# The last two pairs' operands queued behind the last token tile's finish, and its transposes behind the next stage's first product

## The chip, the cores and the metric

The kernel runs on one core of a Trainium2 chip. Its time is device microseconds (us) of one execution, and less is better. TensorE (PE) multiplies, VectorE (DVE) and ScalarE (ACT) work elementwise, GpSimd (POOL) does small operations and issues some DMAs, SyncE (SP) issues most DMAs. Each engine runs its instructions in the order in which they stand in its queue.

## The reference, cut to what matters

The reference is a trunk of two layers on 1024 tokens by 1024 channels in fp32.

```python
h = x
for i in range(DEPTH):
    ...
    if i % N_MIXERS == 0:
        mix = s5_mixer(hn, ...)          # state-space scan, then z @ w_glu, val * sigmoid(gate)
    else:
        mix = shortconv_mixer(hn, ...)   # u @ w_in, gated width-3 conv, @ w_out
    h = h + mix
    h = h + swiglu_ffn(rmsnorm(h, norm_ffn_g[i]), ffn_w_in[i], ffn_w_out[i])
    gate = jax.nn.sigmoid(rmsnorm(h, norm_ple_g[i]) @ ple_w_gate[i])
    h = h + gate * (p[i] @ ple_w_up[i])
return rmsnorm(h, final_norm_g)
```

Ahead of each product stands a norm over the channels, and the product contracts over channels. So the normed tokens have to be transposed before they can be an operand.

## The kernel before, in words

The 1024 tokens are eight tiles of 128, taken in the order 0, 4, 1, 5, 2, 6, 3, 7 (`ORDER`). The last token tile is therefore tile 7. A fp32 product is made of three matmuls of high and low halves (`mm3`, L121 to L124). A high half is an ACT cast (L87), a low half is a DVE subtraction behind it (L88).

**A stage that ends in a norm.** Its products give a tile's `h` (L502 and L503 in `glu`, L433 and L435 in `ple`, L360 in `out_phase`). `square` (L139) sums squares on ACT, `norm_stat` (L144 to L148) makes the factor `rs`, POOL computing the power, and `normed` (L173, DVE) writes the normed tile `xn`. Then PE transposes `xn` in two halves of four 128x128 blocks each (`transposed`, L181).

**A pair.** Three of the stages that follow a norm (the first FFN's input, the convolution's input, the second FFN's input) use `block_product`, seven products for a 2 by 2 block product. Its seven moving operands `c` = 0 to 6 are made by `norm_pair(q)` from tiles `q` and `q + 4`: `c` = 0 and 3 are the two halves of tile `q`, 5 is a half of tile `q + 4`, and 1, 2, 4, 6 are differences T2, T1, T3, T4 (L221 to L232). Each takes a cast and a subtraction. Operands 1 and 2 of the last pair need T1 and T2, and those need the transposes of tile 7. `weights_set` makes seven weight operands `ws` out of two raw loads of 512 KB each (`ra` and `rb`): L275, L276, L278 and L283 are its DVE differences, of which L275 needs both loads.

**The order.** `post(t)` runs after tile t. Before, it runs pair 0 after tile 1, pair 1 after tile 2, pair 2 (tiles 2 and 6) after tile 3, and pair 3 (tiles 3 and 7) after tile 7. A scheduler with priorities orders each engine's queue; `first()` raises an instruction's priority. Products of a block are written 0, 1, 2, 3, ..., and PE's queue takes 0, then 3, then the first matmul each of 1 and 2.

**Slots.** Raw weight loads, the `xn` of the paired stages and the chunks `ch` of hidden activations (one for each token tile in `out_phase`, L346) share four buffers, and they take turns in the order of the program:

```python
if i is None:
    slots.append(slots.pop(0))
```

So a new tile takes the buffer of the fourth allocation before it, and its load waits until the last reader of that one is done. SP issues these loads in its queue's order. `spill` (L236) writes `h` back to DRAM from POOL's queue.

In this document the three places are called S1 (`glu` to the first FFN's input, 400 to 430 us), S2 (`ple` to the convolution's input, 1200 to 1236 us) and S3 (`conv_out`, an `out_phase`, to the second FFN's input, 1545 to 1580 us).

Of the kernel before, what the change touches and what calls it, by code (L numbers as in the profile page):

```python
# [23 lines left out]
def trunk(  # L24
# [107 lines left out]
    def square(t, cs):  # L132

        if "ms" not in squares:
            squares["ms"] = tiny.tile([P, T, 4], F32, name="ms", tag="ms")
        got = squares.setdefault(t, [])
        junk = t2_tile("junk", BF16, D)
        ms = squares["ms"][:, t, len(got):len(got) + 1]
        A.activation(junk[:, cs], h[t][:, cs], AF.Square, scale=1.0 / math.sqrt(D), accum_out=ms)  # L139
        got.append(ms)  # L140

    def norm_stat(t):
# [62 lines left out]
        return uhigh[:, c - 4, kt, l, :]  # L205

    def norm_pair(q, gb):
        t0, t1 = q, q + HT
        halves = 2 if q == HT - 1 else 1
        x0, x1 = normed(t0, gb, halves), normed(t1, gb, halves)  # L210

        def put(c, src):
            split(moving_part(c, 0, q), moving_part(c, 1, q), by_kt(src))

        p11, p12, p22 = transposed(x0, 0), transposed(x1, 0), transposed(x1, 1)
        p21 = transposed(x0, 1, mm)
        put(0, p11)
        b12 = t2_tile("b12")
        A.copy(b12, p12)
        T1 = t2_tile("T1")  # L220
        V.tensor_tensor(T1, b12, p11, ALU.subtract)  # L221
        T2 = t2_tile("T2")
        V.tensor_tensor(T2, p22, T1, ALU.subtract)
        put(1, T2)
        put(2, T1)
        put(3, p21)
        T3 = t2_tile("T3")
        V.tensor_tensor(T3, p22, b12, ALU.subtract)
        put(4, T3)
        put(5, p22)  # L230
        T4 = t2_tile("T4")
        V.tensor_tensor(T4, p21, T2, ALU.subtract)  # L232
        put(6, T4)

    def spill(t):
        nc.gpsimd.dma_start(out=hdram[t], in_=h[t])  # L236
# [52 lines left out]
    def block_product(ws, on_c11=None):  # L289


        def prod(ps, i, start):
            for kt in range(KH):
                sl = slice(kt * P, (kt + 1) * P)
                mm3(ps, ws[i][:, 0, sl], ws[i][:, 1, sl], moving(i, kt, 0), moving(i, kt, 1),
                    start and kt == 0, kt == KH - 1, more=not start)

        a = psum()
        prod(a, 0, True)
        s1 = ev_tile("s1")  # L300
# [25 lines left out]
    def out_phase(wout, groups, last_post, following=()):  # L326
# [6 lines left out]
        for gi, group in enumerate(groups):  # L333
# [5 lines left out]
            for t in ORDER:  # L339
# [10 lines left out]
                for j in parts:  # L350
                    mine = [x[0] for x in group if x[0] // 4 == j]
                    for nb in range(2):
                        cs = slice(nb * 512, (nb + 1) * 512)
                        for ht in mine:
                            ch = parts[j][:, ht % 4]
                            bhi, blo = (w[:, cs] for w in units[ht])
                            mm3(ps[nb], ch[:, 0], ch[:, 1], bhi, blo, ht == group[0][0], ht == group[-1][0])
                        if mine[-1] == group[-1][0]:
                            with first():
                                V.tensor_tensor(h[t][:, cs], ps[nb], h[t][:, cs], ALU.add)  # L360
                                if last:
                                    square(t, cs)
                if soon:
# [52 lines left out]
    def ple(l, units, post):  # L416
        more, makers = ple_units(l, 1, [room_new(i) for i in range(4)])
        for nb in range(2):
# [3 lines left out]
            for t in ORDER:  # L422
# [3 lines left out]
                for c0, c1 in ((0, 256), (256, 512)) if last else ((0, 512),):  # L426
# [4 lines left out]
                    with first():  # L431
                        A.activation(ps, ps, AF.Sigmoid)
                        V.tensor_tensor(upt[:, c0:c1], ps, upt[:, c0:c1], ALU.mult)  # L433
                        hc = slice(nb * 512 + c0, nb * 512 + c1)
                        V.tensor_tensor(h[t][:, hc], upt[:, c0:c1], h[t][:, hc], ALU.add)  # L435
                        square(t, hc)
                if nb == 0 and makers:
                    makers.pop(0)()
# [42 lines left out]
    def glu(post):  # L481
# [3 lines left out]
        for nb in range(4):  # L485
# [8 lines left out]
            for t in ORDER:  # L494
# [5 lines left out]
                with first():  # L500
                    A.activation(sg, ps[:, 256:512], AF.Sigmoid)
                    V.tensor_tensor(sg, ps[:, 0:256], sg, ALU.mult)  # L502
                    V.tensor_tensor(h[t][:, cs], sg, h[t][:, cs], ALU.add)  # L503
                    square(t, cs)
                if nb == 3:
                    post(t)
# [503 lines left out]
    def posted(gain, pairs):  # L1010

        gb = load_gain(gain)

        def pair(q):
            norm_pair(q, gb)
            spill(q)
            spill(q + HT)

        def post(t):
            if not pairs:  # L1020
                return norm_tile(t, gb)
            if 0 < t < HT:
                pair(t - 1)
            if t == T - 1:
                pair(HT - 1)
        return post

    def inner(name, make, bufs, extra=()):
# [71 lines left out]
```

## Time and profile before

| What | Value |
|---|---|
| Time, median of 3 runs | 2356.33 us (2354.39 to 2356.82) |
| The profiled execution's own time | 2359.43 us |
| Its span in the profile | 2357.5 us |
| PE busy | 2247.0 us, 95% |
| DVE busy | 1331.9 us, 56% |
| ACT busy | 765.5 us, 32% |
| POOL busy | 163.1 us, 7% |
| DMA | 288.87 MB moved, mean 123 GB/s |

The profiled execution took 3.10 us longer than the median of the runs. Its span lies 1.9 us below its time; that rest lies outside the span. Busy shares are means over the whole span, and a stage can look quite different.

### The profile page before, as it was taken

The numbers are of one execution on the slowest core, as the hardware profiler recorded it, in microseconds if no ns is written. First come the engines' busy times: TensorE is split into PE (matmuls) and PEld (weight loads), VectorE is DVE, ScalarE is ACT, GpSimd is POOL, SyncE is SP. The second block draws the span as 40 slices with busy tenths as digits, with TensorE's granted clock in tenths as the row PEclk, the third lists the DMA queues.
The fourth block names the chain that finished last, engine by engine and source line by source line (L and its number), as shares of the span: only waits on it lengthen the run. The fifth ranks groups of instructions, "written<-read, shape, count | busy, mean of one in ns | idle before, by whom it ended". The sixth has DMA issues, their size and how long they took to land.

```text
span 2357.5 us, 27090 instructions
## 1 busy us (share of the span) xinstructions
PE 2247.0 (95%) x10253; PEld 1835.7 (78%) x10253; DVE 1331.9 (56%) x2246; ACT 765.5 (32%) x1449; POOL 163.1 (7%) x268
## 2 busy tenths in 40 slices
PE   6888999899999999999979999989999999999998
PEld 4776887788888878878858888768888888788787
DVE  7785326866666642125488776487666666121454
ACT  6554223433333320013343332153333333000232
POOL 2110001000000000000000000010000001000000
PEclk8999999999999999999989999999999999999999
DMA  7555202333333364333232225434333335543333
GB/s 246 141 135 148 69 1 89 105 112 112 111 114 110 107 241 149 118 127 114 70 129 81 90 92 179 159 125 125 108 108 107 111 113 172 212 139 107 108 109 110
DMA packets 212978, 288.87 MB, mean 123 GB/s; under 512 B 21360, under 2 KB 152432, under 8 KB 212848
## 3 DMA queue, kind: packets, MB, share of 16 engines
q1 hardware_dynamic: 191520, 212.63, 29.0%
q0 software_dynamic: 20928, 74.47, 10.2%
q8 instruction: 80, 1.31, 0.2%
q14 instruction: 50, 0.41, 0.1%
q10 hardware_dynamic: 400, 0.04, 0.0%
HBM read 190.93 MB, written 79.69 MB: 115 GB/s over the span
## 4 chain that ended last, share of the span: by engine, by line
PE 85%; DMA 6%; DVE 5%; ACT 1%; SPq 1%; issue 1%; POOL 0%; DVEq 0%; POOLq 0%; ACTq 0%
PE psmm L122 27%; PE psmm L124 27%; PE psmm L123 27%; DMA ch<-hid 2%; PE pstr L181 1%; DMA raw<-in_ffn_w_out_dram 1%; DMA tw<-tmp 1%; DVE W L575 1%; DVE gv L925 1%; DMA h<-hd 1%; DVE tmp L575 1%; DVE ulow L88 1%; DVE uhigh L88 1%; PE pstr L874 0%; DVE raw L575 0%
## 5 line engine op out<-in xcount | busy, mean ns | idle before, releaser
L122 PE MATMUL psmm<-ulow,ws 128*128 128x512 f32 x896 | 351.1, 393 | 1.6 <-ACT s L301 1.6
L123 PE MATMUL psmm<-ulow,ws 128*128 128x512 f32 x896 | 350.6, 391 | 0.0
L124 PE MATMUL psmm<-ulow,ws 128*128 128x512 f32 x896 | 350.4, 391 | 0.0
L124 PE MATMUL psmm<-uhigh,ws 128*128 128x512 f32 x672 | 265.3, 395 | 0.0
L122 PE MATMUL psmm<-uhigh,ws 128*128 128x512 f32 x672 | 265.1, 394 | 0.0
L123 PE MATMUL psmm<-uhigh,ws 128*128 128x512 f32 x672 | 264.9, 394 | 0.0
L360 DVE TENSOR_TENSOR h<-psmm,h 128x512 f32<-128x512 f32 x128 | 88.0, 690 | 276.6 <-PE psmm L124 276.6
L88 DVE TENSOR_TENSOR ws<-raw,ws 128x512 fp32r<-128x512 f32 x224 | 153.6, 688 | 117.8 <-ACT ws L87 117.4
L87 ACT CAST ws<-raw 128x512 fp32r<-128x512 f32 x224 | 137.5, 619 | 213.0 <-PE psmm L124 211.2
L122 PEld LDWEIGHTS psmm<-ulow,ws 128*128 128x128 f32 x896 | 169.4, 189 | 39.5 <-ACT s L301 2.9
L123 PEld LDWEIGHTS psmm<-ulow,ws 128*128 128x128 f32 x896 | 169.4, 189 | 36.2
L124 PEld LDWEIGHTS psmm<-ulow,ws 128*128 128x128 f32 x896 | 169.2, 189 | 36.2
L87 ACT CAST ws<-st 128x512 fp32r<-128x512 f32 x168 | 104.0, 620 | 204.4 <-PE psmm L124 189.5
L123 PEld LDWEIGHTS psmm<-uhigh,ws 128*128 128x128 f32 x672 | 126.1, 188 | 30.3
L124 PEld LDWEIGHTS psmm<-uhigh,ws 128*128 128x128 f32 x672 | 126.1, 188 | 30.3
L122 PEld LDWEIGHTS psmm<-uhigh,ws 128*128 128x128 f32 x672 | 126.1, 188 | 29.1
L323 POOL DMA_DIRECT2D hid<-hs x104 | 78.2, 755 | 903.4 <-DVE hs L88 895.4
L122 PE MATMUL psmm<-ulow,ch 128*128 128x512 f32 x320 | 128.4, 401 | 10.8 <-DMA ch<-hid 10.8
L139 ACT ACTIVATE junk<-h 128x512 bf16<-128x512 f32 (+1 forms) x113 | 64.0, 567 | 204.0 <-DVE h L360 104.0
L87 ACT CAST uhigh<-raw 128x1024 fp32r<-128x1024 f32 x36 | 37.2, 1049 | 278.9 <-PE psmm L124 136.7
L123 PE MATMUL psmm<-ulow,ch 128*128 128x512 f32 x320 | 127.6, 399 | 0.0
L124 PE MATMUL psmm<-ulow,ch 128*128 128x512 f32 x320 | 127.5, 398 | 0.0
(240 smaller groups left out, 4238.5 us busy)
## 6 DMA issues: line engine op xcount, KB each, us to landing
hid<-hs POOLq DMA_DIRECT2D x104, 512.0 KB, 4.3
ch<-hid SPq DMA_DIRECT2D x96, 512.0 KB, 3.7
raw<-in_ffn_w_in_dram SPq DMA_DIRECT2D x88, 512.0 KB, 4.4
raw<-in_ffn_w_out_dram SPq DMA_DIRECT2D x44, 512.0 KB, 3.6
hd<-h POOLq DMA_DIRECT2D x24, 512.0 KB, 3.0
h<-hd SPq DMA_DIRECT2D x24, 512.0 KB, 8.7
raw<-in_conv_w_in_dram SPq DMA_DIRECT2D x24, 512.0 KB, 4.0
up<-ev SPq DMA_DIRECT2D x32, 256.0 KB, 3.2
```

The costliest lines, as they stand in the source:

```text
L87: A.copy(hi, src)
L88: V.tensor_tensor(lo, src, hi.bitcast(F32), ALU.subtract)
L122: PE.matmul(ps, ahi, bhi, start=start, stop=False, skip_group_check=more)
L123: PE.matmul(ps, ahi, blo, start=False, stop=False, skip_group_check=more)
L124: PE.matmul(ps, alo, bhi, start=False, stop=stop, skip_group_check=more)
L139: A.activation(junk[:, cs], h[t][:, cs], AF.Square, scale=1.0 / math.sqrt(D), accum_out=ms)
L181: PE.transpose(pt[:, c * P:(c + 1) * P], xn[:, kt * P:(kt + 1) * P], ident)
L323: nc.gpsimd.dma_start(out=hid[ht // 4][half * HT:(half + 1) * HT, :, ht % 4].rearrange("t p l j -> p t l j"), in_=hs.bitcast(F32))
L360: V.tensor_tensor(h[t][:, cs], ps[nb], h[t][:, cs], ALU.add)
L575: V.tensor_tensor(o, a, b, op)
L925: V.tensor_tensor_scan(gv[:, g, 1:P], dec, sv[:, g, 1:P], 0.0, ALU.mult, ALU.add)
```

## The change

Pairs 2 and 3 are no longer handled apart. At `post(3)` the tiles 2, 6 and 3 are normed. At `post(7)` the new function `last_pairs` norms tile 7 in two halves, transposes tiles 2, 6 and 3, makes the operands of both pairs, and transposes tile 7. All that stands under `issue_after(done["sum"])` and `issue_after(done["square"])`: on DVE and on ACT it comes behind the last tile's sum and square. The transposes of tile 7 are put in `held`, and `block_product` makes them depend, in PE's order, on the last matmul of the next stage's first product. The spills of the four tiles follow.

```diff
+    def others(q, p):
...
+    def last_pairs(xs, gb):
+
+
+        a, z = HT - 2, HT - 1
+        with tc.issue_after(done["sum"]), tc.issue_after(done["square"]):
+            xs[T - 1] = normed(T - 1, gb, 2)
+            p = {(0, 0): transposed(xs[a], 0), (1, 0): transposed(xs[a + HT], 0), (1, 1): transposed(xs[a + HT], 1),
+                 (0, 1): transposed(xs[a], 1, mm)}
+            put(0, a, p[0, 0])
+            r = {(0, i): transposed(xs[z], i, mm) for i in range(2)}
+            put(0, z, r[0, 0])
+            others(a, p)
+            n = len(tc.nc.cur_bb.bb.instructions)
+            r.update({(1, i): transposed(xs[T - 1], i) for i in range(2)})
+            held[:] = [i for i in tc.nc.cur_bb.bb.instructions[n:] if i.engine == PE.engine]
+            others(z, r)
...
         prod(a, 0, True)
+        product = next(i for i in reversed(tc.nc.cur_bb.bb.instructions) if i.engine == PE.engine)
+        while held:
+            tc.add_manual_dep(held.pop(), product.name,
+                              mybir.DependencyInfo(mybir.DependencyClass.NoSync, mybir.DependencyReason.DATA),
+                              reason="behind the first product")
...
         def post(t):
             if not pairs:
                 return norm_tile(t, gb)
-            if 0 < t < HT:
+            if 0 < t < HT - 1:
                 pair(t - 1)
+            if t == HT - 1:
+                xs.update({i: normed(i, gb) for i in (HT - 2, T - 2, HT - 1)})
             if t == T - 1:
-                pair(HT - 1)
+                last_pairs(xs, gb)
+                for i in (HT - 2, T - 2, HT - 1, T - 1):
+                    spill(i)
```

`others(q, p)` holds what `norm_pair` did behind its first `put`: b12, T1, T2, and the operands 1 to 6, in the old order. Lines below the change move down: L275 becomes L295, L276 L296, L278 L298, L283 L303, L360 L385, L433 L458, L435 L460, L346 L371.

In S1, before, PE's queue ends the last tile (`psmm_3570`) and goes on as follows; `xn_3522` is tile 6, `xn_3607` tile 3, `xn_3616` tile 7, and `ws_3685` and `ws_3699` are the weights of products 0 and 3.

```order
L124 MATMUL psmm_3570<-w8_3164,ulow_81 128x512
L181 MATMUL pstr_3529<-ident_72,xn_3522 128x128 x4
L181 MATMUL pstr_3534<-ident_72,xn_3522 128x128 x4
L181 MATMUL psmm_3634<-ident_72,xn_3607 128x128 x4
L181 MATMUL pstr_3619<-ident_72,xn_3607 128x128 x4
L181 MATMUL pstr_3624<-ident_72,xn_3616 128x128 x4
L181 MATMUL pstr_3629<-ident_72,xn_3616 128x128 x4
L122 MATMUL psmm_3712<-ulow_81,ws_3685 128x512
...
L124 MATMUL psmm_3712<-ulow_81,ws_3685 128x512
L122 MATMUL psmm_3712<-ulow_81,ws_3699 128x512
```

In S1, of the change, the same place; `xn_3514` is tile 2, `xn_3522` tile 6, `xn_3530` tile 3, `xn_3569` tile 7, `ws_3684` and `ws_3698` are the weights of products 0 and 3.

```order
L124 MATMUL psmm_3532<-w8_3164,ulow_81 128x512
L181 MATMUL pstr_3572<-ident_72,xn_3514 128x128 x4
L181 MATMUL psmm_3587<-ident_72,xn_3514 128x128 x4
L181 MATMUL pstr_3577<-ident_72,xn_3522 128x128 x4
L181 MATMUL pstr_3582<-ident_72,xn_3522 128x128 x4
L181 MATMUL psmm_3594<-ident_72,xn_3530 128x128 x4
L181 MATMUL psmm_3599<-ident_72,xn_3530 128x128 x4
L122 MATMUL psmm_3711<-ulow_81,ws_3684 128x512
...
L124 MATMUL psmm_3711<-ulow_81,ws_3684 128x512
L181 MATMUL pstr_3628<-ident_72,xn_3569 128x128 x4
L181 MATMUL pstr_3633<-ident_72,xn_3569 128x128 x4
L122 MATMUL psmm_3711<-ulow_81,ws_3698 128x512
```

The transposes of tile 7 (the last two rows with L181) moved from ahead of product 0 to between products 0 and 3, and the eight of tile 2 moved behind the last tile's matmuls.

In S2, before, DVE's queue has these rows around the last tile's sum (`h_6783` is tile 3, `h_6784` tile 7, `raw_9135` and `raw_9137` the loads of the next stage's first weights):

```order
L435 TENSOR_TENSOR h_6783<-upt_8930,h_6783 128x512
...
L275 TENSOR_TENSOR st_9142<-raw_9135,raw_9137 128x512
L88 TENSOR_TENSOR ulow_81<-T1_8998,ulow_81 128x4x128
L232 TENSOR_TENSOR T4_9014<-psmm_8989,T2_9000 128x512
...
L433 TENSOR_TENSOR upt_9020<-psmm_9022,upt_9020 128x512
...
L435 TENSOR_TENSOR h_6784<-upt_9020,h_6784 128x512
```

In S2, of the change, on DVE (`h_6782` is tile 3, `h_6783` tile 7, `raw_9133` and `raw_9135` the same two loads):

```order
L460 TENSOR_TENSOR h_6782<-upt_8929,h_6782 128x512
L146 TENSOR_TENSOR ms_7819<-ms_7819 128x1
L173 SCALAR_TENSOR_TENSOR xn_8977<-h_6782,rs_8975,gb_8343 128x1024
L295 TENSOR_TENSOR st_9140<-raw_9133,raw_9135 128x512
L458 TENSOR_TENSOR upt_8979<-psmm_8981,upt_8979 128x512
L296 TENSOR_TENSOR raw_9135<-raw_9135 128x512
L460 TENSOR_TENSOR h_6783<-upt_8979,h_6783 128x512
```

The weights' difference that needs both loads now stands directly ahead of the last tile's L458 and sum, with none of pair 2's operands between.

In S3, on SP, the last chunk is followed by the next stage's four loads; before, `raw_11645` and `raw_11647` are `ra` and `rb` of its first block, `raw_11785` and `raw_11787` those of its second.

```order
L346 DMA ch_11443<-hid1_100 128x1024
L346 DMA ch_11535<-hid1_100 128x1024
L100 DMA raw_11647<-in_ffn_w_in_dram 128x8x128
L100 DMA raw_11645<-in_ffn_w_in_dram 128x8x128
L100 DMA raw_11785<-in_ffn_w_in_dram 128x8x128
L100 DMA raw_11787<-in_ffn_w_in_dram 128x8x128
```

Of the change (`raw_11642` and `raw_11644` are the first block's, `raw_11782` and `raw_11784` the second's):

```order
L371 DMA ch_11441<-hid1_100 128x1024
L371 DMA ch_11493<-hid1_100 128x1024
L100 DMA raw_11782<-in_ffn_w_in_dram 128x8x128
L100 DMA raw_11642<-in_ffn_w_in_dram 128x8x128
L100 DMA raw_11644<-in_ffn_w_in_dram 128x8x128
L100 DMA raw_11784<-in_ffn_w_in_dram 128x8x128
```

The chunk of tile 7 keeps its place in the queue, but its buffer is another one. Before, the allocations ahead of it are the chunks of tiles 6 and 3 and the `xn` of tiles 2 and 6, so it takes the buffer of tile 6's chunk. Of the change, the `xn` of tile 3 comes ahead of it too, and it takes the buffer of tile 3's chunk. The second block's `ra` moved ahead of the first block's loads.

In S3, before, DVE's queue has the last pair's T2 ahead of the second block's L275:

```order
L221 TENSOR_TENSOR T1_11607<-b12_11605,pstr_11583 128x512
L88 TENSOR_TENSOR ws_11657<-st_11655,ws_11657 128x512
L223 TENSOR_TENSOR T2_11609<-pstr_11593,T1_11607 128x512
...
L275 TENSOR_TENSOR st_11792<-raw_11785,raw_11787 128x512
L88 TENSOR_TENSOR ulow_81<-T2_11609,ulow_81 128x4x128
```

Of the change, T2 stands behind it:

```order
L221 TENSOR_TENSOR T1_11602<-b12_11600,psmm_11556 128x512
L295 TENSOR_TENSOR st_11789<-raw_11782,raw_11784 128x512
L88 TENSOR_TENSOR ws_11667<-st_11652,ws_11667 128x512
L88 TENSOR_TENSOR ws_11670<-raw_11644,ws_11670 128x512
L88 TENSOR_TENSOR ws_11786<-raw_11782,ws_11786 128x512
L223 TENSOR_TENSOR T2_11604<-pstr_11595,T1_11602 128x512
```

`raw_11784` takes the buffer of tile 7's `xn`, so its load waits for tile 7's transposes, which PE's queue now has behind product 0.

## Rows read from the trace of the kernel before

**Rows 1.** The page's first part, busy time and share of each engine.

```profile
PE 2247.0 (95%) x10253; PEld 1835.7 (78%) x10253; DVE 1331.9 (56%) x2246; ACT 765.5 (32%) x1449; POOL 163.1 (7%) x268
```

**Rows 2.** Waits in the whole span: us in total, times, longest.

```profile
PE pstr L181 <- DVE xn L173: 36.0, 5, 10.7
```

**Rows 3.** Windows: length, busy of PE, PEld, DVE, ACT, POOL, clock, DMA, GB/s.

```profile
409.00:414.00 5.00, 0.00 (x0) 0.00 (x0) 5.00 (x10) 3.09 (x7) 0.00 (x0) 0.95 0.74 204
414.00:419.00 5.00, 0.04 (x1) 0.05 (x1) 4.22 (x9) 2.30 (x6) 1.13 (x2) 0.50 0.19 79
```

**Rows 4.** Timeline in S1: start us, duration us, instruction, count, idle before it.

```profile
400.20 0.60 PE L181 MATMUL pstr<-ident,xn 128*128 128x128 f32 x4
...
400.99 0.48 PE L122 MATMUL psmm<-w,ulow 128*128 128x512 f32 x1
...
406.32 0.39 PE L124 MATMUL psmm<-w,ulow 128*128 128x512 f32 x1
...
418.95 1.97 PE L181 MATMUL pstr<-ident,xn 128*128 128x128 f32 x8 [10.42 <-DVE xn L173]
...
420.58 0.78 PE L122 MATMUL psmm<-ulow,ws 128*128 128x512 f32 x1
...
422.00 0.62 ACT L87 CAST ws<-st 128x512 fp32r<-128x512 f32 x1 [0.77 <-DVE st L283]
...
427.35 0.68 DVE L223 TENSOR_TENSOR T<-pstr,T 128x512 f32<-128x512 f32 x1
...
427.95 0.68 DVE L228 TENSOR_TENSOR T<-pstr,b 128x512 f32<-128x512 f32 x1
...
428.74 0.96 PE L122 MATMUL psmm<-ulow,ws 128*128 128x512 f32 x3
```

**Rows 5.** The first two weight loads of S3 (1557.2, 1558.0): issue to landing.

```profile
DMA to landing us min/median/max: 4.4/5.8/7.1
```

**Rows 6.** The same for the four weight loads in S1.

```profile
DMA to landing us min/median/max: 3.8/4.4/4.9
```

**Rows 7.** Timeline in S2, columns as in rows 4.

```profile
1205.97 0.39 PE L124 MATMUL psmm<-w,ulow 128*128 128x512 f32 x1
...
1232.37 0.68 DVE L223 TENSOR_TENSOR T<-pstr,T 128x512 f32<-128x512 f32 x1
...
1233.83 0.89 PE L122 MATMUL psmm<-ulow,ws 128*128 128x512 f32 x3
```

**Rows 8.** Chunk loads ahead of S3's last two tiles, issue to landing.

```profile
L346 SPq DMA_DIRECT2D ch<-hid x2: 319/320/320, 1537.8 to 1545.1; - x2
...
DMA to landing us min/median/max: 3.3/3.4/3.4
```

**Rows 9.** Timeline in S3, columns as in rows 4.

```profile
1550.30 0.39 PE L124 MATMUL psmm<-w,ch 128*128 128x512 f32 x1
...
1551.32 0.48 PE L122 MATMUL psmm<-w,ch 128*128 128x512 f32 x1
...
1556.74 0.40 PE L124 MATMUL psmm<-w,ch 128*128 128x512 f32 x1
...
1572.72 0.68 DVE L223 TENSOR_TENSOR T<-pstr,T 128x512 f32<-128x512 f32 x1
...
1579.11 0.39 PE L122 MATMUL psmm<-ulow,ws 128*128 128x512 f32 x1
```

**Rows 10.** PE's timeline behind three other waits for a chunk.

```profile
1479.82 0.47 PE L122 MATMUL psmm<-ulow,ch 128*128 128x512 f32 x1 [2.20 <-DMA ch<-hid]
...
2018.07 0.80 PE L122 MATMUL psmm<-ulow,ch 128*128 128x512 f32 x1 [3.45 <-DMA ch<-hid]
...
2021.20 0.39 PE L123 MATMUL psmm<-ulow,ch 128*128 128x512 f32 x1
...
1045.66 0.80 PE L122 MATMUL psmm<-w,ch 128*128 128x512 f32 x1 [4.24 <-DMA ch<-hid]
...
1051.79 0.40 PE L124 MATMUL psmm<-w,ch 128*128 128x512 f32 x1
```

More of the change, by code (lines that the diff above doesn't have):

```diff
@@ L138, in square @@
         ms = squares["ms"][:, t, len(got):len(got) + 1]
-        A.activation(junk[:, cs], h[t][:, cs], AF.Square, scale=1.0 / math.sqrt(D), accum_out=ms)
+        done["square"] = A.activation(junk[:, cs], h[t][:, cs], AF.Square, scale=1.0 / math.sqrt(D), accum_out=ms).ins
         got.append(ms)
@@ L207, in norm_pair @@
     def norm_pair(q, gb):
[L208 to L217, printed above, removed]
+        x0, x1 = normed(q, gb), normed(q + HT, gb)
+        p = {(0, 0): transposed(x0, 0), (1, 0): transposed(x1, 0), (1, 1): transposed(x1, 1), (0, 1): transposed(x0, 1, mm)}
@@ L218, in norm_pair, with put @@
+        put(0, q, p[0, 0])
+        others(q, p)
+    def put(c, q, src):
+        split(moving_part(c, 0, q), moving_part(c, 1, q), by_kt(src))
+    def others(q, p):
         b12 = t2_tile("b12")
-        A.copy(b12, p12)
+        A.copy(b12, p[1, 0])
         T1 = t2_tile("T1")
-        V.tensor_tensor(T1, b12, p11, ALU.subtract)
+        V.tensor_tensor(T1, b12, p[0, 0], ALU.subtract)
         T2 = t2_tile("T2")
-        V.tensor_tensor(T2, p22, T1, ALU.subtract)
-        put(1, T2)
-        put(2, T1)
@@ L226, in norm_pair @@
-        put(3, p21)
+        V.tensor_tensor(T2, p[1, 1], T1, ALU.subtract)
+        put(1, q, T2)
+        put(2, q, T1)
+        put(3, q, p[0, 1])
         T3 = t2_tile("T3")
-        V.tensor_tensor(T3, p22, b12, ALU.subtract)
-        put(4, T3)
-        put(5, p22)
+        V.tensor_tensor(T3, p[1, 1], b12, ALU.subtract)
+        put(4, q, T3)
+        put(5, q, p[1, 1])
         T4 = t2_tile("T4")
-        V.tensor_tensor(T4, p21, T2, ALU.subtract)
-        put(6, T4)
+        V.tensor_tensor(T4, p[0, 1], T2, ALU.subtract)
@@ new lines, in others @@
+        put(6, q, T4)
+    done = {}
+    held = []
+    def last_pairs(xs, gb):
[12 more added lines that the diff above has]
+            others(z, r)
@@ L359, in out_phase @@
                             with first():
-                                V.tensor_tensor(h[t][:, cs], ps[nb], h[t][:, cs], ALU.add)
+                                done["sum"] = V.tensor_tensor(h[t][:, cs], ps[nb], h[t][:, cs], ALU.add).ins
                                 if last:
@@ L434, in ple @@
                         hc = slice(nb * 512 + c0, nb * 512 + c1)
-                        V.tensor_tensor(h[t][:, hc], upt[:, c0:c1], h[t][:, hc], ALU.add)
+                        done["sum"] = V.tensor_tensor(h[t][:, hc], upt[:, c0:c1], h[t][:, hc], ALU.add).ins
                         square(t, hc)
@@ L502, in glu @@
                     V.tensor_tensor(sg, ps[:, 0:256], sg, ALU.mult)
-                    V.tensor_tensor(h[t][:, cs], sg, h[t][:, cs], ALU.add)
+                    done["sum"] = V.tensor_tensor(h[t][:, cs], sg, h[t][:, cs], ALU.add).ins
                     square(t, cs)
```

1 line of the change is left out of this document (added).

## The prediction

> **What bounds the kernel now.** I read the busy shares first. PE is busy for 95% of the span [rows 1], so a change can win only idle time of PE, or time at its lower clock. Then I looked for that idle time in the waits. PE waits 36.0 us in five waits for the normed tile `xn` [rows 2], and they lie in S1, S2 and S3. One of them is the 10.42 us ahead of tile 7's transposes in S1 [rows 4]. The change goes for exactly these. So the next question is what DVE does meanwhile. From 409 to 414 us DVE is busy for all of the 5.00 us, while PE has nothing to do; its clock is 0.95 there and 0.50, which is 1.2 of 2.4 GHz, in the next 5 us [rows 3]. The reader should see that PE waits for a long row of DVE operations and not for a single late one. Taking away PE's wait doesn't shorten that row. So I measure the change at the point where PE can't go on without the row's end: the first matmul of product 1. It needs the cast of the last pair's T2, and the order has products 0 and 3 ahead of it in both kernels. In S1 T2 starts at 427.35 and this matmul at 428.74 [rows 4]. In S2 these are 1232.37 and 1233.83 [rows 7]. What is behind that point is nearly the same in both queues, and PE then has work without such waits, so a shift there carries to the end.
>
> **Prices.** DVE starts a 128x512 operation 0.60 us after the one before (427.35 and 427.95), and it takes 0.68 [rows 4]. An ACT cast of that size takes 0.62 [rows 4]. Where DVE needs the cast of a difference that it has just made, it loses 0.68 + 0.62 less the 0.60 that it would have taken anyway, and something between engines, about 0.8 us. For the two halves of an `xn` I take two 0.60 and 0.13 for a third operand, 1.33, an estimate. PE starts matmuls every 0.236 us (24 from 1551.32 to 1556.74) [rows 9]. Behind a wait of 3.45 us the next 7 took 3.13 us instead of 7 x 0.236 = 1.65; behind one of 4.24 us, 14 took 6.13 instead of 3.30; behind one of 2.20 us the first took 0.47 and they weren't slowed [rows 10]. So a new wait of some 3 us costs 0 to 2.8 us more in clock.
>
> **S1: a small gain.** The eight transposes of tile 2 go behind the last tile, whose matmuls then start at 400.20 instead of 400.99 [rows 4], and end near 405.75 (the last started at 406.32 before [rows 4], 0.8 earlier now, and 0.23 on). Sum, square, the first cast and then the first operand row (`ulow` from tile 2) follow some 2.5 us later, at 408.25; I estimate these from sigmoid, product and sum of 256 columns and the ACT work behind them. From that row to T2, 26 operations stand in the changed queue, one of them the `xn` of tile 7. That is 25 x 0.60 + 1.33 = 16.3, so T2 would start at 424.6. Two waits come into that row. The difference L295 needs both weight loads, and four loads now go out close together: in S3, where they did so before, two of them took 4.4 and 7.1 us [rows 5], in S1 they take 3.8 to 4.9, median 4.4 [rows 6]. With 7.1 the second load lands at 414.7, 0.9 us after its turn; with 4.4 it is no wait. The weights' cast behind L298 stops DVE for 0.8. T2 starts at 426.3 and its cast is ready 1.3 later, at 427.6, 1.1 us earlier than 428.74. The first weights' subtraction is the 12th operation of the row and done at 417.2, so PE does product 0 from there instead of from 420.58 [rows 4]. At the lower clock it is through with product 3 by 424.5 and so waits 3 us there: 0 to 1.5 more in clock, and I take 0.6. Term: -0.5, between -2.8 (no waits, no clock) and +0.4.
>
> The Trainium skill ("DMA: Bandwidth & Descriptors", section "Issuing engines are not separate DMA queues") says that DMAs of all issuing engines run on the same 16 DMA engines and interleave. That speaks against the change, which puts four spills of POOL's queue beside four weight loads of SP's. The landings agree, up to 7.1 us in S3 against 4.9 in S1 [rows 5, 6]. By that rule S1 keeps its -0.5 and the sum below stays; by S1's own median of 4.4 the term would be -1.4 and the sum 0.9 less.
>
> **S2: a small loss.** Here the wait is added. L295 stands directly ahead of the last tile's L458 and sum, and its second load takes the buffer of tile 6's `xn`, which PE now reads only behind the last tile's matmuls. These end at 1206.2 before [rows 7] and 0.8 earlier now, as in S1, and tile 6's `xn` should be there by 1206.6, an estimate. Behind L295 in DVE's queue stand L458, the sum, tile 7's `xn` and both pairs' operands, and PE waits for these. The load goes out near 1207.7 and lands 4.4 to 7.1 us later [rows 5], so L295 starts between 1212.1 and 1214.8. The last tile's `upt` load stands behind it in SP's queue and may cost up to 1.1 more. The sum is 1.8 behind L295, and from the sum to T2 stand 29 operations, two of them on single columns and one `xn`, which also waits about 0.5 for square and `rs`: 26 x 0.60 + 1.33 + 0.2 + 0.5 = 17.6. T2 starts between 1231.5 and 1235.3, against 1232.37 [rows 7]. I take 0.9 late. PE has done product 3 by about 1231 and waits some 3 us: 0 to 2.8 in clock, I take 1.2. Term: +2.1, between -0.9 and +5.7.
>
> **S3: the loss.** The chunk of tile 7 takes the buffer of tile 3's chunk, so it goes out when tile 3's last matmul is done (started 1550.30 [rows 9]), about 1550.75, and not at 1545.1 [rows 8]. It needs 3.4 us [rows 8] and lands at 1554.2. Before, the tile's first matmul started at 1551.32 [rows 9]: 2.9 us. The wait that PE sees is about 3.1 us, as only four transposes remain in it; the clock costs 0 to 2.8, and I take 0.9. Behind this wait on PE stand the tile's 24 matmuls, all transposes and product 0, so all of S3 is +3.8 late. The wait of the chunk on SP holds up the weight loads behind it too, but these need buffers that come free later anyway.
>
> From the end E' of the last tile's matmuls (before: E = 1556.98) I walk again. The first operand row comes at E' + 2.4. Up to T2 stand 28 operations and one of them is the `xn`: 27 x 0.60 + 1.33 = 17.5, which gives E' + 19.9. L295 of the second block stands four operations ahead of T2. It needs the load into the buffer of tile 7's `xn`, whose transposes stand behind product 0. Product 0 needs the first weights, which land near E' + 8.1 (issue at 1.0, 7.1 more [rows 5]), starts behind their cast and subtraction at E' + 9.4 and runs at the lower clock first (0.45 apart [rows 10]), to E' + 14. The transposes end at E' + 14.9 and the load lands 4.4 later. So L295 starts at E' + 19.3, T2 at E' + 21.7 and its cast is ready at E' + 23.0. With the two first matmuls of products 1 and 2, 26 matmuls are done at E' + 23.5. Before they were done at 1579.11 [rows 9], which is E + 22.1: 1.4 more. T2 itself stood at 1572.72 [rows 9], so it goes from E + 15.7 to E' + 21.7, because pair 2's operands and three weight rows now stand ahead of it. Term: 3.8 + 1.4 = +5.2. If the loads land in 4.4 and the clock holds, T2 follows at E' + 19.9 and this is +2.5; with the clock at its worst +7.1.
>
> **Edits at nothing.** The held transposes cost PE the same wherever they stand; they lie ahead of product 3, whose weights come later than they end. The spills stand in POOL's queue behind the last `rs`, and POOL is busy for 7% [rows 1]; without that cover each would delay a hidden store by an issue. The square is the old one.
>
> **The sum.** -0.5 + 2.1 + 5.2 = +6.8 us. On the profiled execution's 2359.43 that is 2366.2. It took 3.1 more than the median, so I put the sum on the median, 2356.33: 2363.1.
>
> **Rivals.**
> *A, the other side: the waits on `xn` go and PE starts earlier for good.* Product 0 starts 3.4 us earlier in S1 (417.2 against 420.58 [rows 4]), by the same walk some 3 in S2 and 1 in S3. If T2 is there when product 3 ends, all of it stays: -7.4, 2348.9. What decides is whether T2 starts before 424 in S1. Against it speaks that DVE was already full at 5.00 of 5.00 [rows 3], and the count of 26 operations; for it, that the waits of 36.0 us are really gone. Even these are not worth 36, since DVE's row behind them remains.
> *B, no change that can be told.* The chunk's wait is real but short of the clock, L295 in S2 isn't late, and loads land in 4.4: -1.4 + 0.3 + 2.5 = +1.4, 2357.7. For it speaks that S1's loads landed so [rows 6].
> *C, worse: each of the new waits also puts the clock back.* Then S1 is +0.4, S2 +3.7 and S3 +7.1: +11.2, 2367.5. The waits of 3.45 and 4.24 us speak for it, that of 2.20 against it [rows 10]. The Trainium skill ("TensorE: Matmul & The Clock Gate", section "HAM oscillation — how this bites in real kernels") describes such a case, where waits for DMAs between short runs of matmuls put the clock back each time; it would give C's time.
> *D, the change doesn't do what it says.* The queues show that it does, so I give it nothing.
>
> **How the numbers follow.** I give 0.50 to my sum, 0.12 to A, 0.23 to B and 0.15 to C. The time is that of the sum. The range goes from 2354 (all three terms at their low ends give -1.2, and a little of A) to 2369 (C, with S2 nearer its high end). That leaves out most of A and little above. A measurement of this kernel can tell about 0.2%, 4.7 us, from no change. My sum lies 2.1 above that bound; of its 0.50 I count 0.37 as slower and 0.13 as the same. With C, 0.52 slower; with B, 0.36 the same; A gives 0.12 faster.
>
> **What would show it.** In the changed kernel's trace, the 10 us waits on `xn` should be gone. In S3 PE should wait some 3 us for a chunk ahead of the last tile, with the next matmuls 0.45 apart if the clock fell. DVE should wait for a weight load ahead of the last sum in S2 and ahead of T2 in S3. T2 should start near 426.3 and 1233, and 21.7 us after the last tile's matmuls in S3. The prediction is wrong if PE goes from product 3 to product 1 without a wait, or if the last chunk lands before tile 3's matmuls end.

## The result, and the profile after

The changed kernel took 2365.18 us (median of 6 runs, 2361.92 to 2369.22), the kernel before 2357.72 beside it (6 runs, 2354.39 to 2361.44). The ratio is 1.0034, with a 95% interval of 1.002 to 1.0047, which is 4.7 to 11.1 us. I had put it at 2363.1.

The page's first part, the counterpart of [rows 1]: PE is busy 8 us longer, with as many instructions, so part of the loss is matmuls that run slowly.

```profile
PE 2255.0 (95%) x10253; PEld 1840.8 (78%) x10253; DVE 1331.5 (56%) x2243; ACT 764.8 (32%) x1449; POOL 163.9 (7%) x268
```

PE's waits over the whole span of the kernel after (us in total, times, longest). The 36.0 us for `xn` of [rows 2] have shrunk to 3.3. In their place PE waits for the weights' casts, for the cast of T2 (`ulow`) and for the weights' low halves.

```profile
PE psmm L122 <- DMA ch<-hid: 21.5, 7, 4.1
PE psmm L122 <- ACT ws L87: 20.7, 4, 9.1
...
PE psmm L124 <- DVE ws L88: 5.1, 3, 3.3
PE psmm L122 <- ACT ulow L87: 4.8, 3, 3.5
...
PE psmm L181 <- DVE xn L173: 3.3, 1, 3.3
```

**S1.** The timeline of the kernel after (columns as in rows 4). The last tile's matmuls end at 401.84, where the first transposes start; call it E'. Before, that end E was 406.32 + 0.23 = 406.55 [rows 4].

```profile
401.84 0.60 PE L181 MATMUL pstr<-ident,xn 128*128 128x128 f32 x4
...
407.92 0.50 PE L122 MATMUL psmm<-ulow,ws 128*128 128x512 f32 x1 [3.30 <-ACT ws L87]
...
410.14 0.69 DVE L295 TENSOR_TENSOR st<-raw 128x512 f32<-128x512 f32 x1
...
412.69 0.79 PE L124 MATMUL psmm<-ulow,ws 128*128 128x512 f32 x1 [3.27 <-DVE ws L88]
...
421.74 0.68 DVE L223 TENSOR_TENSOR T<-pstr,T 128x512 f32<-128x512 f32 x1
...
423.13 0.97 PE L122 MATMUL psmm<-ulow,ws 128*128 128x512 f32 x3 [1.07 <-ACT ulow L87]
```

Product 0 starts at E' + 6.08, well ahead of the old E + 14.03 (420.58 [rows 4]). But then it stands still for 3.27 us in its third matmul, and products 0 and 3 are spread out until T2 comes. Product 1's first matmul starts at E' + 21.29, before at E + 22.19 (428.74): 0.90 earlier. The end E' itself is earlier by the 0.9 of the moved transposes. The windows over the same stretch (columns as in rows 3) show why there was no more to win: DVE is as full as it was in [rows 3].

```profile
404.00:409.00 5.00, 1.22 (x8) 0.66 (x6) 4.68 (x9) 4.11 (x8) 0.82 (x2) 1.00 0.95 296
409.00:414.00 5.00, 1.73 (x4) 1.21 (x5) 4.90 (x9) 1.72 (x3) 0.00 (x0) 0.52 0.45 125
```

**S2.** The timeline of the kernel after; the last tile's matmuls end at 1197.97, before at 1206.20 [rows 7].

```profile
1197.97 0.60 PE L181 MATMUL pstr<-ident,xn 128*128 128x128 f32 x4
...
1199.04 1.75 SPq L100 DMA_DIRECT2D raw<-in_conv_w_in_dram  x2
...
1200.88 0.53 SPq L449 DMA_DIRECT2D upt<-up  x1
...
1207.67 0.69 DVE L295 TENSOR_TENSOR st<-raw 128x512 f32<-128x512 f32 x1 [4.07 <-DMA raw<-in_conv_w_in_dram]
...
1208.28 0.68 DVE L458 TENSOR_TENSOR upt<-psmm,upt 128x512 f32<-128x512 f32 x1
...
1209.48 0.68 DVE L460 TENSOR_TENSOR h<-upt,h 128x512 f32<-128x512 f32 x1
...
1227.16 0.68 DVE L223 TENSOR_TENSOR T<-pstr,T 128x512 f32<-128x512 f32 x1
...
1228.55 1.65 PE L122 MATMUL psmm<-ulow,ws 128*128 128x512 f32 x3 [3.52 <-ACT ulow L87]
...
1231.70 0.47 PE L124 MATMUL psmm<-ulow,ws 128*128 128x512 f32 x1
```

DVE stands 4.07 us in front of L295, and the last tile's sum waits behind it. T2 starts at E' + 29.19, before at E + 26.17 [rows 7]. PE then waits 3.52 us for its cast, and the matmuls behind that wait run slowly until 1231.70. The window there (columns as in rows 3) has a granted clock of 0.53, where 0.50 is 1.2 of 2.4 GHz:

```profile
1229.00:1232.00 3.00, 3.00 (x8) 2.30 (x8) 3.00 (x7) 1.20 (x3) 0.00 (x0) 0.53 0.08 22
```

The load of `upt`, too, stands on SP behind the two weight loads. Its issue to landing:

```profile
DMA to landing us min/median/max: 7.4/7.4/7.4
```

1200.88 + 7.4 is 1208.28, where L458 starts. So this load held the sum as long as L295 did.

**S3.** The timeline of the kernel after:

```profile
1548.35 0.60 PE L181 MATMUL pstr<-ident,xn 128*128 128x128 f32 x4
1548.54 0.32 SPq L371 DMA_DIRECT2D ch<-hid  x1
...
1551.97 0.50 PE L122 MATMUL psmm<-w,ch 128*128 128x512 f32 x1 [3.02 <-DMA ch<-hid]
...
1552.81 0.63 PE L122 MATMUL psmm<-w,ch 128*128 128x512 f32 x1
...
1559.20 1.03 PE L181 MATMUL pstr<-ident,xn 128*128 128x128 f32 x8
...
1569.66 0.69 DVE L295 TENSOR_TENSOR st<-raw 128x512 f32<-128x512 f32 x1 [1.38 <-DMA raw<-in_ffn_w_in_dram]
...
1578.85 0.68 DVE L295 TENSOR_TENSOR st<-raw 128x512 f32<-128x512 f32 x1
...
1581.26 0.68 DVE L223 TENSOR_TENSOR T<-pstr,T 128x512 f32<-128x512 f32 x1
...
1582.64 1.31 PE L122 MATMUL psmm<-ulow,ws 128*128 128x512 f32 x3 [0.22 <-ACT ulow L87]
```

The chunk of tile 7 goes out 0.19 us after tile 3's last matmul, and PE waits 3.02 us for it. The matmuls from 1552.81 to 1555.80 start 0.43 apart, and the window over them has a granted clock of 0.59. The last tile ends at 1559.20, and T2 starts 22.06 later.

```profile
1552.00:1556.00 4.00, 4.00 (x11) 3.18 (x12) 1.28 (x1) 0.00 (x0) 0.00 (x0) 0.59 0.19 79
```

**The stages in one table.** I worked these out from the start times of the matmuls in each trace, transposes left out: from the 73rd matmul ahead of the next stage's first product to the 91st of that stage. Before, S1, S2 and S3 took 56.58, 61.94 and 56.39 us on this measure. S3 is split at the last matmul ahead of the product. Differences to before, in us:

| Kernel | S1 | S2 | S3 | of it last tile | behind it |
|---|---|---|---|---|---|
| after | -1.82 | +3.74 | +6.52 | +4.40 | +2.11 |
| e1_s1_only | -1.52 | +0.46 | +1.13 | +0.01 | +1.12 |
| e2_s2_only | +0.09 | +3.02 | +1.69 | +0.01 | +1.69 |
| e3_s3_only | +0.20 | -0.03 | +6.47 | +4.24 | +2.23 |
| e4_slot | -1.41 | +3.10 | +1.39 | -0.43 | +1.82 |
| e5_st_behind | -1.19 | +3.56 | +8.34 | +5.70 | +2.64 |
| e6_upt | -1.15 | +1.97 | +6.53 | +4.09 | +2.44 |
| e7_no_hold | -0.11 | +5.35 | +8.85 | +4.35 | +4.50 |
| e8_t2_first | +1.73 | +2.14 | -0.04 | -0.42 | +0.38 |
| e9_s1_s3slot | -0.49 | -0.07 | +0.11 | -0.42 | +0.54 |
| e10_chunk | +0.03 | -0.08 | +3.99 | +4.14 | -0.15 |
| e11_s1_again | -0.61 | +0.05 | +0.12 | +0.01 | +0.11 |
| e12_late_spill | -1.29 | +0.03 | +0.95 | 0.00 | +0.95 |

The rows that a kernel leaves as before show how far to trust a single trace: S1 and S2 repeat within 0.5 us, while S3 unchanged lies between +0.12 and +1.69. For the kernel after the three add up to +8.44. The profiled spans differ by less (2362.7 and 2357.5), because the profiled execution of before took 0.8 to 5.1 us longer than all others ahead of S1 (3.8 longer than that of the kernel after), where nothing was changed. The medians differ by 7.46.

### The profile page after: what moved, and what is told of

It is laid out like the page before. It is cut to its first block, busy times and chain, and to the rows that moved or that the text cites. A ratio compares the mean times of both kernels' runs of the same rounds, so it can differ in the third digit from the quotient of the medians.

```text
span 2362.7 us, 27084 instructions
## 1 busy us (share of the span) xinstructions
PE 2255.0 (95%) x10253; PEld 1840.8 (78%) x10253; DVE 1331.5 (56%) x2243; ACT 764.8 (32%) x1449; POOL 163.9 (7%) x268
## 4 chain that ended last, share of the span: by engine, by line
PE 85%; DMA 6%; DVE 6%; SPq 1%; ACT 1%; issue 1%; POOL 0%; DVEq 0%; POOLq 0%; ACTq 0%
PE psmm L122 27%; PE psmm L124 27%; PE psmm L123 27%; DMA ch<-hid 2%; PE pstr L181 1%; DMA tw<-tmp 1%; DMA raw<-in_ffn_w_out_dram 1%; DMA h<-hd 1%; DVE W L600 1%; DVE gv L950 1%; DMA raw<-in_ffn_w_in_dram 1%; DVE uhigh L88 0%; DVE tmp L600 0%; PE pstr L965 0%; DVE ws L88 0%
## 5 line engine op out<-in xcount | busy, mean ns | idle before, releaser
L385 DVE TENSOR_TENSOR h<-psmm,h 128x512 f32<-128x512 f32 x128 | 88.0, 690 | 269.4 <-PE psmm L124 269.4
L122 PEld LDWEIGHTS psmm<-ulow,ws 128*128 128x128 f32 x896 | 170.7, 191 | 65.7 <-ACT ws L87 21.7
L123 PE MATMUL psmm<-uhigh,ch 128*128 128x512 f32 x320 | 126.5, 395 | 1.0 <-DVE uhigh L88 1.0
```

The source lines that it names most:

```text
L122: PE.matmul(ps, ahi, bhi, start=start, stop=False, skip_group_check=more)
L123: PE.matmul(ps, ahi, blo, start=False, stop=False, skip_group_check=more)
L385: done["sum"] = V.tensor_tensor(h[t][:, cs], ps[nb], h[t][:, cs], ALU.add).ins
```

## The experiments

**One stage at a time.** A switch puts the old order back in the stages that aren't tried. For S1 alone:

```diff
-    def posted(gain, pairs):
+    def posted(gain, pairs, late=True):
...
-            if 0 < t < HT - 1:
+            if 0 < t < HT - 1 or not late and t == HT - 1:
                 pair(t - 1)
-            if t == HT - 1:
+            if late and t == HT - 1:
...
-            if t == T - 1:
+            if t == T - 1 and not late:
+                pair(HT - 1)
+            elif t == T - 1:
                 last_pairs(xs, gb)
...
-            ple(l, units, posted(norm_mix_g[l + 1], True))
+            ple(l, units, posted(norm_mix_g[l + 1], True, False))
...
-    conv_out(posted(norm_ffn_g[1], True))
+    conv_out(posted(norm_ffn_g[1], True, False))
```

> The change in S1 alone; S2 and S3 keep the queues of before. Theory (the three stages add up, S1 gains a little, S3 loses by the chunk's buffer): 1 to 2 us faster than before, which is about 0.9993; from the last tile's matmuls to the first matmul of product 1 some 21 us instead of 23. Rival (the operands queued behind the last tile and the held transposes cost the same in every stage): about 2.5 us slower.

Measured: 2352.65 us, ratio 0.9976 (0.9966 to 0.9986), S1 1.52 shorter. Faster than both kernels here; e11 below puts a limit on that.

S2 alone has `False` in the calls of S1 and S3.

> The change in S2 alone. Theory: 1 to 3 us slower than before (T2 hardly later, but PE waits 3 to 4 us for its cast and runs at the lower clock behind it). Rival (same cost in every stage): about 2.5 us slower, so this run alone does not tell them apart.

Measured: 2360.28 us, ratio 1.0013 (1.0004 to 1.0021), S2 3.02 longer.

S3 alone has it in those of S1 and S2.

> The change in S3 alone. Theory: 5 to 8 us slower than before, with a wait of 3 us for a chunk ahead of the last tile and its first matmuls 0.43 us apart. Rival (same cost in every stage): about 2.5 us slower.

Measured: 2364.38 us, ratio 1.0027 (1.0017 to 1.0038), S3 6.47 longer. So each stage keeps its sign by itself, and the loss is that of S2 and S3.

**The chunk's buffer.** Here the changed kernel allocates the `xn` of tile 3 behind the last chunk, so that the chunk gets back the buffer of tile 6's chunk:

```diff
-                xs.update({i: normed(i, gb) for i in (HT - 2, T - 2, HT - 1)})
+                xs.update({i: normed(i, gb) for i in (HT - 2, T - 2)})
             if t == T - 1:
+                xs[HT - 1] = normed(HT - 1, gb)
                 last_pairs(xs, gb)
```

> The whole change, but tile 3's normed tile is allocated behind the last tile's chunk, so that in S3 this chunk takes the buffer of tile 6's chunk again, as before. Theory: the wait for the chunk and the lower clock behind it go, some 4 us, so 2 to 4 us slower than before instead of 7 to 8. Rival (the chunk's wait is hidden by what DVE has to do anyway): no better than the whole change, 6 to 8 us slower.

Measured: 2359.07 us, ratio 1.0004 (0.9995 to 1.0013). PE's timeline ahead of S3's last tile shows no wait left; the first matmul stands directly behind four transposes:

```profile
1547.03 0.60 PE L181 MATMUL pstr<-ident,xn 128*128 128x128 f32 x4
1547.39 0.48 PE L122 MATMUL psmm<-w,ch 128*128 128x512 f32 x1
```

The other way round, the kernel before gets nothing but the early allocation in S3:

```diff
+            if early3 and t == HT - 1:
+                xs[HT - 1] = normed(HT - 1, gb, 2)
```

> The kernel before in everything but one thing: in S3 the xn of tile 3 is allocated right behind tile 3, ahead of tile 7's chunk, so that this chunk takes the buffer of tile 3's chunk. Operands, transposes and DVE's order stay. Theory (the chunk's buffer is the whole loss of S3): PE waits 2.9 to 3.1 us for the chunk ahead of the last tile, the tile's matmuls then run partly at the lower clock, its matmuls end 4 to 5 us later and the time is +4 to +6 us, ratio 1.0015 to 1.0025. Rival (the old order has slack behind the last tile, as PE waits some 10 us for the xn of tile 7 there and the late tile costs no more than DVE's row): the end of the last tile is late by as much, but T2 follows it sooner, and the time is +2 or less.

Measured: 2359.85 us, ratio 1.0014 (1.0004 to 1.0024). The timeline of PE and SP:

```profile
1545.63 0.60 PE L181 MATMUL pstr<-ident,xn 128*128 128x128 f32 x4
...
1545.82 0.32 SPq L373 DMA_DIRECT2D ch<-hid  x1
...
1549.17 0.77 PE L122 MATMUL psmm<-w,ch 128*128 128x512 f32 x1 [2.51 <-DVE xn L173]
```

The wait is put down to an `xn`, which was done within 0.03 us of the chunk's landing. But the chunk went out at 1545.82 and took 3.2 us to land, at 1549.04, so PE could not have started before. The last tile ends 4.14 us late, and behind it nothing is given back (-0.15). So the rival, that the old 10 us wait on `xn` would swallow the delay, falls: that wait is DVE's row, and the row starts as late as the tile ends. One buffer's turn costs 4 us.

**What the order itself is worth in S3.** S1 and S3 as in e4, S2 in the old order.

> S1 and S3 in the changed order, with tile 3's xn allocated behind the last chunk, and S2 in the old order. Theory (S1 wins 1.5 us, S3 costs nothing once the chunk has its old buffer, S2 is the rest of the loss): S1 -1.4, S2 +0.3, S3 +1.3 by the kernels with single stages, so -2 to -4 us in all, ratio 0.9985, PE's waits on xn gone in S1 and S3, and no wait for a chunk ahead of S3's last tile. Rival (the chunk's buffer was not all, the order in S3 itself costs): S3 +3 or more, ratio 1.000 or above. If the changed order is worth something in S3 too, S3 is below -1 and the ratio below 0.998.

Measured: 2354.09 us, ratio 0.9994 (0.9985 to 1.0003), S3 +0.11. With the buffer put back, e4's trace has S3 at +1.39 and this one at +0.11, both within what S3 does unchanged. So the new order in S3 has no cost and no gain that these traces can tell.

**S2: L295 or the `upt` load.** First L295 was moved behind the sum:

```diff
-        V.tensor_tensor(s3, a11, a21, ALU.subtract)
+        if held:
+            with tc.issue_after(done["sum"]):
+                V.tensor_tensor(s3, a11, a21, ALU.subtract)
+        else:
+            V.tensor_tensor(s3, a11, a21, ALU.subtract)
```

> The whole change, but in S2 the weights' difference L295 is queued behind the last tile's sum. Theory (the last tile's upt load, which stands behind the second weight load in SP's queue, lands at the same time as that weight load, so L295's wait only covers it): S2 gains 0.6 us at most, time as for the whole change, 7 us slower than before. Rival, as in the prediction (L295's wait is what makes the sum late): the sum comes some 4 us earlier and the kernel is 3 to 5 us faster than the whole change.

Measured: 2365.08 us, ratio 1.0036 (1.0024 to 1.0047), S2 +3.56 against +3.74. The wait only changed its name. DVE's timeline shows it at the product with `upt`:

```profile
1208.87 0.69 DVE L462 TENSOR_TENSOR upt<-psmm,upt 128x512 f32<-128x512 f32 x1 [4.17 <-DMA upt<-up]
```

Then, without that edit, the `upt` load was put ahead of the two weight loads on SP. The scheduler now also put the sum ahead of L295, so this kernel takes both waits away from the sum:

```diff
-                nc.sync.dma_start(out=upt, in_=updram[l][:, t, cs])
+                done["upt"] = nc.sync.dma_start(out=upt, in_=updram[l][:, t, cs]).ins
...
+        with tc.issue_after(done.pop("upt")) if "upt" in done else ExitStack():
             ra = load_raw(src_a, "p (kt n) -> p kt n", kt=KT)
             rb = load_raw(src_b, "p (kt n) -> p kt n", kt=KT)
```

> The whole change, but in S2 the last tile's upt load is queued on SP ahead of the next stage's two weight loads; by the planner the sum then stands ahead of L295 too. Theory (the load behind the weight loads is what delays the sum): the sum comes some 7 us earlier, T2 3 to 5 us earlier, the wait of 3.5 us for its cast shrinks and the clock does not fall behind it, 3 to 5 us faster than the whole change. Rival (L295 alone counts, or DVE's row is full anyway): less than 1 us.

Measured: 2363.47 us, ratio 1.003 (1.0018 to 1.0042). The timeline in S2:

```profile
1204.62 0.69 DVE L461 TENSOR_TENSOR h<-upt,h 128x512 f32<-128x512 f32 x1
...
1223.24 0.69 DVE L296 TENSOR_TENSOR st<-raw 128x512 f32<-128x512 f32 x1 [1.44 <-DMA raw<-in_conv_w_in_dram]
1223.85 0.68 DVE L223 TENSOR_TENSOR T<-pstr,T 128x512 f32<-128x512 f32 x1
...
1225.23 1.65 PE L122 MATMUL psmm<-ulow,ws 128*128 128x512 f32 x3 [3.00 <-ACT ulow L87]
...
1231.60 0.55 PE L124 MATMUL psmm<-ulow,ws 128*128 128x512 f32 x1
```

The sum comes 4.9 us earlier (1209.48 before this edit), though the last tile ended 0.4 us later in this execution. Of that T2 keeps 3.3: 1.44 goes into a wait of the second block's difference (here L296) for its load. T2 is now even a little earlier behind the last tile than in the kernel before, at E' + 25.49 against E + 26.17. But PE still waits 3.00 for the cast, and the matmuls behind it run 0.43 apart until 1231.60, at a granted clock of 0.51:

```profile
1225.00:1232.00 7.00, 6.49 (x15) 4.64 (x16) 7.00 (x13) 2.66 (x6) 0.00 (x0) 0.51 0.28 78
```

From product 1's first matmul to the 91st of the stage this kernel takes 18.67 us, the kernel after 16.75 and the kernel before 15.04. So S2 wins only 1.8 of the kernel after's 3.74. Part of the gain that I had expected went into that load's wait, the rest was given back by the clock, and what is left of S2's loss is the clock's.

**The hold.** The transposes of tile 7 are not held behind product 0.

```diff
-            n = len(tc.nc.cur_bb.bb.instructions)
...
-            held[:] = [i for i in tc.nc.cur_bb.bb.instructions[n:] if i.engine == PE.engine]
```

> The whole change, but the transposes of tile 7 are not held behind the first product. Theory (the hold is worth nothing either way, since PE waits for weights while the normed tile is long there): within 1.5 us of the whole change, each of the three stages within 1 us. Rival (the hold carries the change): 2 us or more slower than the whole change.

Measured: 2366.57 us, ratio 1.004 (1.0027 to 1.0053). In its trace each stage is 1.6 to 2.3 us longer than in the kernel after, more than I had given it. PE waits in front of those transposes, most of all in S2, with product 0 queued behind them; in its waits:

```profile
PE pstr L181 <- ACT ulow L87: 9.0, 2, 7.7
```

The intervals of the two ratios overlap, so the runs alone don't prove a loss. Nor is its cause shown. Behind the last tile, product 0 starts only 0.5 us later in S2 than in the kernel after, and no later in S1 (E' + 5.98 against E' + 6.08). The scheduler also ordered DVE's row anew: in S1 T2 comes 3.3 us earlier (E' + 16.61 against E' + 19.91), and product 3 starts 1.7 later (E' + 18.84 against E' + 17.15).

**T2 first.** On top of e4, pair 2's operands 4 to 6 and the weights of products 4 to 6 go behind the last pair's T2:

```diff
-            others(a, p)
+            T3T4 = differences(a, p, *early(a, p))
...
-            others(z, r)
+            e = early(z, r)
+            with tc.issue_after(done["T2"]):
+                last(a, p, *T3T4)
+                later(z, r, *e)
```

`early` holds `others` up to operand 3, `differences` T3 and T4, `last` and `later` the operands 4 to 6.

> As e4_slot, and DVE and ACT make the last pair's T2 ahead of pair 2's operands 4 to 6 and of the first block's weights of products 4 to 6. Theory (the row of DVE operations up to T2 sets the end of each stage): T2 comes 3 to 5 us earlier, S1 gains 1 us and S2 4 to 5 us with the clock, so 4 to 6 us faster than e4_slot and 3 to 5 us faster than before. Rival (PE, the clock or the weight loads bound the stages): within 1.5 us of e4_slot.

Measured: 2358.93 us, ratio 1.001 (1.0001 to 1.0018): no better than e4, a miss. PE's timeline in S1:

```profile
423.20 0.61 PE L122 MATMUL psmm<-ulow,ws 128*128 128x512 f32 x2
...
426.00 0.50 PE L123 MATMUL psmm<-ulow,ws 128*128 128x512 f32 x1 [2.18 <-DVE ulow L88]
...
426.86 0.63 PE L123 MATMUL psmm<-ulow,ws 128*128 128x512 f32 x1
```

The high half of T2 no longer stops PE, but its low half, a DVE operation further down the row, does so for 2.18 us, and then the matmuls run 0.43 apart. S1 went from -1.41 in e4 to +1.73. T2 itself came only 1.2 us sooner there (E' + 19.15 against E' + 20.32), not 3 to 5, since ahead of it DVE waited 1.49 us for a weight load and 1.66 us for an ACT copy.

**S1 again, and its load.** The kernel of e1 once more:

> The kernel with the changed order in S1 alone, once more, beside fresh runs of the kernel before. Theory (S1's new order wins some 1.5 us; the 0.9976 of its first comparison holds more than that): ratio 0.9985 to 0.9997, the S1 stretch 1 to 2 us shorter. Rival 1 (S1 is worth all of the 0.24%): ratio 0.997 to 0.9985. Rival 2 (nothing in it, the S1 stretch varies by more than its gain from execution to execution): ratio 0.9997 or above.

Measured: 2353.5 us, ratio 0.9993 (0.9984 to 1.0002), S1 0.61 shorter. So e1's 0.9976 was partly luck, and a gain of S1 alone is some 0.1%, about what can be told at all. DVE's timeline says where S1 differs between the two traces, first e1, then e11:

```profile
410.70 0.69 DVE L296 TENSOR_TENSOR st<-raw 128x512 f32<-128x512 f32 x1 [0.39 <-DMA raw<-in_ffn_w_in_dram]
```

```profile
411.63 0.69 DVE L296 TENSOR_TENSOR st<-raw 128x512 f32<-128x512 f32 x1 [1.30 <-DMA raw<-in_ffn_w_in_dram]
```

That wait is 0 in the kernel after, 0.39 in e1, 0.50 in e4, 1.30 in e11 and 1.43 in e9, and S1 is shorter by 1.82, 1.52, 1.41, 0.61 and 0.49. In e5 and e6, which leave S1 as in the kernel after, it is 0.71 and 0.74, with S1 shorter by 1.19 and 1.15. Each of the seven pairs adds up to 1.8 to 1.9. So S1's new order is worth 1.9 us less a wait for one load.

Last, S1 alone with the spill of tile 7 on SP's queue, behind the third weight load, and not on POOL's beside the first two:

```diff
-                for i in (HT - 2, T - 2, HT - 1, T - 1):
+                for i in (HT - 2, T - 2, HT - 1):
...
+            with tc.issue_after(loads[-2]):
+                nc.sync.dma_start(out=hdram[T - 1], in_=h[T - 1])
```

> The kernel with the changed order in S1 alone, and there the spill of tile 7 no longer goes out from GpSimd beside the next stage's first two weight loads but from SP behind the third load. In five traces the gain of S1 plus the wait of L295 for its load came to 1.8 to 1.9 us each time, so this wait (0 to 1.4 us) is what makes S1's gain vary. Theory (the spill on the same DMA engines makes the loads late): the loads' median goes from 6.2 to 7.6 us back to 4.4 to 5.5, L295 waits nothing, the S1 stretch is 1.8 to 1.9 shorter, ratio 0.9985 to 0.9995. Rival (the loads slow one another, the spill matters little): landings as before, L295 waits up to 1.4, S1 0.4 to 1.9 shorter.

Measured: 2354.05 us, ratio 0.9991 (0.9981 to 1.0), S1 1.29 shorter. The three weight loads, issue to landing, and the difference that needs two of them:

```profile
DMA to landing us min/median/max: 3.9/6.2/7.0
```

```profile
411.43 0.69 DVE L298 TENSOR_TENSOR st<-raw 128x512 f32<-128x512 f32 x1 [1.23 <-DMA raw<-in_ffn_w_in_dram]
```

The loads did not return to a median of 4.4 [rows 6]. The longest landing fell from 8.2 (e11) to 7.0, and the second load's, which the difference waits for, from 7.4 to 6.2; but that was 6.2 in the kernel after too, with the spill beside it. The spill's packets ran from 410.60 on, behind most of the loads', so three loads together are slow without it. How much the spill adds stays open. The wait itself can't be compared with the seven: the scheduler moved L298 forward by two operations, its turn came 4.4 us behind the first operand row where it was 5.6 in e11, and wait and gain add up to 2.5 here.

## Why the prediction was right

Sign, size and the pattern over the stages came out: a small gain, a small loss, a large loss, in all +6.8 forecast and +7.46 measured in medians. That the sum is so near is in part luck: S1 came out 1.3 us below its term, S2 1.6 and S3 1.3 above theirs, in traces that add up to +8.44. Step by step:

**S1, the term mis-sized.** I took -0.5, the trace shows -1.82. The row of 26 operations was right: with the 0.9 wait for the load and 0.6 for the clock taken out, my walk gives -2.0, and the runs show 1.9 less that wait. The wait of 0.9 lies within the 0 to 1.43 of seven traces; the kernel after had none. The clock's 0.6 did not come: PE waited 1.07 us ahead of product 1, not 3, since product 0 had stood still and run slowly earlier.

The Trainium skill ("DMA: Bandwidth & Descriptors", section "Issuing engines are not separate DMA queues") says that DMAs of all issuing engines interleave on the same 16 DMA engines. I had taken that as a reason for slower landings beside the spills. The landings were slower (medians of 6.2 to 7.6 us against 4.4 [rows 6]). But three loads now went out within 2 us of each other, before at most two, and in e12, with the spill behind them, the median was still 6.2. So the traces don't show the spill as the cause.

**S2, mis-sized and with half of its cause.** I took +2.1, measured are +3.0 to +3.7. The sum stood 1.8 behind L295 and T2 17.7 behind the sum, as counted (17.6). What was off is the time of L295: it started 9.7 us behind the last tile's matmuls, where my 0.9 late meant 8.5. Its second load went out 2.4 us behind them, about as counted, but took 7.1 us, the top of my range, where the 0.9 stands for 6.2. T2 was so 2.1 late (29.19 - 26.17 less 0.91 for the earlier end) and not 0.9, and the clock took 1.7, not 1.2. I had named the `upt` load as something that "may cost up to 1.1 more"; e5 shows that it holds the sum by itself, and e6 that the sum comes 4.9 us earlier when neither that load nor L295 is in its way. The clock is the other half: in e6, with T2 as early as before, it cost 3.6 us, more than the 2.8 that I had put as its most.

**S3, right in sum, with its parts shifted.** I took 3.8 for the chunk and 1.4 behind it; measured are 4.40 and 2.11, or 4.14 for the chunk alone (e10). The wait was 3.02 as forecast, and the clock took more than my 0.9: the last tile is 2.83 us late at its first matmul and 4.40 at its last, so 1.6. Behind it T2 came at E' + 22.06 (forecast 21.7), but not for the reason given. The second block's L295 found its load there: it was issued at 1574.10 and took 3.9, so it landed 0.9 before L295's turn at 1578.85. In its place the first block's L295 waited 1.38 for its load and DVE 0.68 for the weights' cast. Both products ran at the lower clock to their ends, and PE then waited only 0.22 for T2's cast. But it is T2's row that set the end: in e4 product 3 ran at 2.4 GHz, PE waited 2.48 us for the cast, and product 1 started at E' + 23.51, against E' + 23.44 here. With unchanged S3 rows at up to +1.69 behind the tile, not much of it can be called the change's.

**The hold.** I put it at nothing. Without it (e7) each stage's trace was 1.6 to 2.3 us longer, so that step was not borne out; how much of this is the hold's own stays open.

**The rivals.** A fell as argued: the waits on `xn` went, and PE waits for weights and T2 in their place. B fell too: behind the chunk's wait the clock was low, and L295 in S2 was late. C's clock came in S2 and S3, not in S1. The Trainium skill ("TensorE: Matmul & The Clock Gate", section "HAM oscillation — how this bites in real kernels") describes that loss. In these traces matmuls ran at 1.2 GHz behind the waits of 3.00 (e6), 3.02 and 3.52 us, and at 2.4 GHz behind that of 1.07. The length of the wait alone doesn't tell which: in S3 they ran at 1.2 GHz behind one of 2.29 us (e6) and at 2.4 GHz behind one of 2.48 (e4).

## What to carry to other kernels

An engine's long wait may be the shadow of another engine's row of work: before moving work into the wait, count that row from end to end, since its length and not the wait is what can be won. Where buffers take turns, follow the turns when an allocation moves; here one earlier `xn` shifted one chunk load by 3 us and cost 4 us, more than the reordering won in any stage. And a small load that stands behind large ones in a queue can be as late as they are (`upt` took 7.4 us to land behind two weight loads, and 2.6 ahead of them in e6), so look at the queue's order before blaming the instruction that seems to wait.

## What was not expected of the hardware

Three weight loads of 512 KB that go out within 2 us landed after 3.9 to 8.4 us (S1), and the wait for the second ran from 0 to 1.43 us from execution to execution, where S1's new order is worth 1.9. On SP's queue the spill's issue held the queue for 3.14 us (e12), where a weight load's takes 0.38. And a wait of some 3 us cost 1.6 us (the chunk in S3) to 3.6 us (e6 in S2) more in slow matmuls behind it, so that shortening the work ahead of it won little in e6, where the wait stayed.
